# Relative-position rows written in eight pieces at a later place, and a new order of the feed-forward chunks, in a two-block transformer kernel

## The chip, the cores and the metric

The kernel runs on one core of a Trainium2 chip. The metric is the time of one execution on the device in microseconds (us); lower is better. Each measurement is the median of several runs.

## The reference, cut to what matters

Two transformer blocks run one after the other on 256 positions of width 2048, all in fp32. The first has a causal convolution branch, attention with a forgetting gate, gates, and a feed-forward part of width 8192. The second has attention with a relative-position bias, a pooling branch, and a gated feed-forward part of width 5632 with a short convolution. What the change touches:

```python
# first block
h = rmsnorm(x, g_mlp)
u = square(relu(h @ w_ff1))                  # 2048 -> 8192
x = x + u @ w_ff2                            # 8192 -> 2048
# second block
bias_own = rel_bias[:, rel_bucket(q_pos - k_pos)]        # 8 heads, 32 buckets
s_own = where(q_pos >= k_pos, q @ k.T * scale + bias_own, NEG)
...
u = h @ w_up                                 # 2048 -> 2 * 5632
gate, val = split(conv_b + causal_conv3(u, conv_w))
x = x + (silu(gate) * val) @ w_down          # 5632 -> 2048
```

The bias depends only on the head and on the distance of the two positions, so a row of 383 values for each head holds all of it, and a tile with one query per partition is that row shifted by one element from partition to partition.

## The kernel before, in words

**Chunks.** All the large products are one long list of chunks (`add_chunk`, line 137). A chunk makes 256 x 512 outputs in one PSUM tile (`acc`, two buffers). It has one weight tile of 512 x 512 for each 512 rows of the contraction, and each of these has four k steps of 128 rows. The activations stand transposed in tiles of the pool `kk` (11 buffers, line 79); they and the weights are split in a high and a low fp32r part, and a k step is three products (high-high, low-high, high-low) for two halves of the positions: six matmuls of 128x512 (`both`, line 882). A feed-forward chunk has four weight tiles, so 16 k steps.

**Weights.** `fetch` (line 831) loads a weight tile of 1 MB from SP's queue into one of four `raw` buffers, four tiles ahead of its use. `split_unit` (line 840) splits half a tile (a unit, two k steps) three units ahead: ScalarE casts (`wh`, line 846), VectorE subtracts (`wl`, line 847). The main loop (line 898) emits for each unit the split of a later unit, at the second unit of a tile also a fetch, then the two k steps.

**Tasks.** Everything else is emitted between k steps. The variable `now` counts k steps; `later(delay, fn)` (line 93) puts a function in a heap with a due time, and after every k step `run_due` (line 107) emits at most three that are due, the earliest due first and, of equal ones, the one put in first. `chain` (line 97) puts in several with a gap between. `need(key)` (line 112) runs tasks until a key is ready. The order of emission is the order in which each engine's queue runs; engines and queues wait on one another only through the data. `before[i]` runs a function where chunk i begins.

**Feed-forward, first block** (lines 787 to 793). Four times: four chunks of the first layer, `u0` to `u3` and so on, each from the four `f` tiles; then four chunks of the second layer, each of which takes the four `u` tiles in order, and each of which is added into x. A `u` chunk is emptied by `evac_ff` (line 559): ScalarE applies Relu, a task one step later squares, tasks from two steps later on transpose on VectorE (`turned`, line 180: 16 transposes, three to a task, line 190), and `split_out` (line 147) writes the high part on ScalarE (line 155) and the low part on VectorE (line 162). So the fourth `u` tile is made while the second layer's first chunk already uses the first three. `close_block` after the last of these blocks makes the second block's activations.

**Feed-forward, second block** (lines 811 to 820): the same shape with pairs of chunks (gate and value) of `w_up` that make `d0` to `d10`, in groups of 4, 4 and 3, and four `w_down` chunks behind each group.

**Relative-position rows** (lines 629 to 645). At k step 40, in the first block's projections, POOL's queue loads a one-hot table `oh` (33 x 384) and the bias table `rb` (33 x 8). 18 steps later a matmul `p_b` (line 638) makes the 8 rows of 383 values, VectorE copies them to `e` (8 partitions, line 640), and one DMA from POOL's queue (line 642) writes each row 128 times to DRAM, 1024 rows in all, with a stride of 513 floats for the shift. Much later `rel_bias_tiles` (line 647, called from the second block's `k2_done`) reads them back with a stride of 512 as bias tiles `k_nb`, four DMAs from POOL's queue.

Of the kernel before, what the change touches and what calls it, by code (L numbers as in the profile page):

```python
# [11 lines left out]
F32 = mybir.dt.float32  # L12
# [7 lines left out]
P = 128  # L20
# [3 lines left out]
NH = 8  # L24
W1 = 1024
FF1 = 8192
FF2 = 5632
EPS = 1e-6
NEG = -1e30
CW = 512  # L30
# [31 lines left out]
def tile_two_blocks(  # L62
# [5 lines left out]
    nc = tc.nc  # L68
    V, S, TE = nc.vector, nc.scalar, nc.tensor

    def pool(name, bufs, space=None):
        kw = {"space": space} if space else {}
        return ctx.enter_context(tc.tile_pool(name=name, bufs=bufs, **kw))
# [7 lines left out]
    s_p = pool("s", 2)  # L81
    pt_p = pool("pt", 3)
    bg_p = pool("bg", 2)
    st_p = pool("st", 4)
    dr_p = pool("dr", 1, DRAM)
# [7 lines left out]
    def later(delay, fn, *keys):  # L93
        seq[0] += 1
        heapq.heappush(tasks, (now[0] + delay, seq[0], fn, keys))

    def chain(delay, stages, *keys, gap=1):

        for i, fn in enumerate(stages):
            later(delay + i * gap, fn, *(keys if i == len(stages) - 1 else ()))  # L100
# [11 lines left out]
    def need(*keys):  # L112
        for key in keys:
            while key not in ready:
                run_one()
# [19 lines left out]
    chunks, before = [], {}  # L135

    def add_chunk(w, row0s, c0, ncol, acts, evac):

        chunks.append((w, row0s, c0, ncol, acts, evac))
# [61 lines left out]
    def group_keys(key):  # L201
        return [f"{key} {j}" for j in range(4)]
# [21 lines left out]
    def squares(part, n):  # L224
        for tb in range(TB):
            junk = s_p.tile([P, CW], F32, tag="s", name="junk")
            S.activation(junk, xs[n][:, tb, :], AF.Square, accum_out=part[:, tb, n:n + 1])  # L227
# [13 lines left out]
    def to_acts(name, n, gcol, delay):  # L241

        key = f"{name}{n}"
        def use(b, p):
            return split_out(key, 2 * b, 2, p, [gcol[:, 4 * n + 2 * b + i:4 * n + 2 * b + i + 1] for i in range(2)])
        if name == "h" or n == 3:
            transposed(xs[n], use, delay if name == "h" else delay + 3, group_keys(key), lag=0, step=0)
        else:
            turned(xs[n], use, delay, group_keys(key), rate=2, lag=3)
# [53 lines left out]
    AT = {}  # L303
# [73 lines left out]
    hT = lambda name: [f"{name}{n}" for n in range(4)]  # L377
# [57 lines left out]
    def evac_scaled(rname, then, mult=None):  # L435

        def evac(acc):
            z = z_p.tile([P, TB, CW], F32, tag="z", name="z")
            for tb in range(TB):
                S.activation(z[:, tb, :], acc[:, tb, :], AF.Copy, scale=R[rname][:, tb:tb + 1])  # L440
            then(z)
        return evac
# [94 lines left out]
    def evac_add(n, then=None):  # L537
        def evac(acc, tb=None):
            if tb is not None:
                V.tensor_tensor(out=xs[n][:, tb, :], in0=xs[n][:, tb, :], in1=acc, op=OP.add)  # L540
                nc.sync.dma_start(outr[:, tb, n * CW:(n + 1) * CW], xs[n][:, tb, :])
                return
            V.tensor_tensor(out=xs[n], in0=xs[n], in1=acc, op=OP.add)
            if then:
                then(n)
        return evac

    def next_acts(name, gfn, part, rname):
        def then(n):
            if n == 0:  # L550
                need("vcol")
            to_acts(name, n, gfn(), 2)
            squares(part, n)
            if n == 3:
                R[rname] = rstd_of(part, rname)
        return then


    def evac_ff(key):
        def evac(acc):  # L560
            z = z_p.tile([P, TB, CW], F32, tag="z", name="z_f")
            for tb in range(TB):
                S.activation(z[:, tb, :], acc[:, tb, :], AF.Relu, scale=R["r2"][:, tb:tb + 1])
            later(1, lambda: S.activation(z, z, AF.Square))
            turned(z, lambda b, p: split_out(key, 2 * b, 2, p), 2, group_keys(key))
        return evac
# [44 lines left out]
    def k2_done(half):  # L611
# [14 lines left out]
                head_task(2, h, 12 + 7 * i)  # L626
        return then

    def rel_bias_rows():
        oh = s_p.tile([33, 384], F32, tag="s", name="oh")  # L630
        nc.gpsimd.dma_start(oh, cst[0:33, C_OH:C_OH + 384])
        rb = const.tile([33, NH], F32, name="rb")
        nc.gpsimd.memset(rb[32:33, :], 1.0)
        nc.gpsimd.dma_start(rb[0:32, :], rel_bias_2.rearrange("h b -> b h"))

        def task():
            p = tr_p.tile([P, 512], F32, tag="tr", name="p_b")
            TE.matmul(p[0:8, 0:384], rb, oh, start=True, stop=True)
            e = s_p.tile([NH, 384], F32, tag="s", name="e")
            V.tensor_copy(e, p[0:8, 0:384])  # L640
            ed = dr_p.tile([NH, P * CW], F32, name="ed")
            nc.gpsimd.dma_start(bass.AP(tensor=ed.tensor, offset=ed.offset, ap=[[P * CW, NH], [CW + 1, P], [1, 383]]),
                                e[:, None, 0:383].to_broadcast([NH, P, 383]))
            AT["ed"] = ed
        later(18, task, "ed")

    def rel_bias_tiles():
        need("ed")
        ed = AT["ed"]
        for half in range(2):  # L650
            nb = k_p.tile([P, 4, MAXCOL], F32, tag="k", name="k_nb")
            o = ed.offset + half * 4 * P * CW + 127
            for c0, o, n in ((0, o + P, P), (P, o, T)):
                nc.gpsimd.dma_start(nb[:, :, c0:c0 + n],
                                    bass.AP(tensor=ed.tensor, offset=o, ap=[[CW, P], [P * CW, 4], [1, n]]))
            AT[2, "nb", half] = nb

    def v2_done(half):
# [70 lines left out]
    def evac_up(which, j, key):  # L729
        def then(z):  # L730
            cv = z_p.tile([P, 4, T], F32, tag="z", name="z_cv")

            def use(b, p):
                a = cv[:, 2 * b:2 * b + 2, :]
                c0 = (0 if which == "g" else 44) + 4 * j + 2 * b
                steps = conv3(a, p, lambda i, t: ccol[:, t, c0 + i:c0 + i + 1], lambda i: ccol[:, 3, c0 + i:c0 + i + 1])
                if which == "v":
                    g = FU["g", j][:, 2 * b:2 * b + 2, :]
                    need(f"gate{j} {2 * b}")
                    return steps + [lambda: V.tensor_tensor(out=a, in0=a, in1=g, op=OP.mult), *split_out(key, 2 * b, 2, a)]  # L740
                t = {}

                def sigmoid():
                    t["s"] = s_p.tile([P, 2, T], F32, tag="s", name="sg")
                    S.activation(t["s"], a, AF.Sigmoid)
                return steps + [sigmoid, lambda: V.tensor_tensor(out=a, in0=a, in1=t["s"], op=OP.mult)]
            if which == "g":
                FU["g", j] = cv
            if which == "g":
                turned(z, use, 2, group_keys(f"gate{j}"), rate=2)  # L750
            else:
                soon = j == FF2 // CW - 1
                transposed(z, use, 2 if soon else 3, group_keys(key), gap=1 if soon else 2)
        return then
# [4 lines left out]
    G4 = [0, 512, 1024, 1536]  # L759
# [24 lines left out]
    for n in range(4):  # L784
        add_chunk(w_mix_out[0], G4, n * CW, CW, hT("mg"),
                  evac_add(n, next_acts("f", lambda: vcol[:, VEC["g_mlp"], :], part1, "r2")))
    for blk in range(4):
        for i in range(4):
            j = 4 * blk + i
            add_chunk(w_ff1[0], G4, j * CW, CW, hT("f"), evac_ff(f"u{j}"))  # L790
        for n in range(4):
            add_chunk(w_ff2[0], [(4 * blk + i) * CW for i in range(4)], n * CW, CW, [f"u{4 * blk + i}" for i in range(4)],
                      evac_add(n, close_block if blk == 3 else None))
    wi2 = w_in_2[0]
    for half in range(2):
        add_chunk(wi2, G4, 2 * W1 + half * CW, CW, hT("i"), v2_done(half))
# [11 lines left out]
    def store(n):  # L808
        nc.sync.dma_start(outr[:, :, n * CW:(n + 1) * CW], xs[n])

    j = 0
    for cnt in (4, 4, 3):
        js = list(range(j, j + cnt))
        j += cnt
        for jj in js:
            add_chunk(w_up_2[0], G4, jj * CW, CW, hT("g"), evac_scaled("r4", evac_up("g", jj, f"d{jj}")))
            add_chunk(w_up_2[0], G4, FF2 + jj * CW, CW, hT("g"), evac_scaled("r4", evac_up("v", jj, f"d{jj}")))
        for n in range(4):
            add_chunk(w_down_2[0], [jj * CW for jj in js], n * CW, CW, [f"d{jj}" for jj in js],
                      evac_add(n, store if j == 11 else None))  # L820


    wtiles = []
# [53 lines left out]
        later(4 * n + 3, lambda n=n: squares(part0, n))  # L877
    later(16, first_rstd, "r1")
    later(18, load_vectors)
    later(40, rel_bias_rows)  # L880

    def both(k, kt, wh, wl, stop):

# [77 lines left out]
```

## Time and profile before

| | us |
|---|---|
| median of 3 runs | 2394.24 (2393.58 to 2395.01) |
| the profiled execution | 2393.52 |
| its span in the trace | 2391.8 |
| TensorE (PE) busy in it | 2362.4 |
| VectorE (DVE) busy | 1662.8 |
| ScalarE (ACT) busy | 1159.0 |
| GpSimd (POOL) busy | 36.7 |

The profile is one execution; times in it are us from its first instruction unless ns is said. PE is TensorE's matmuls, PEld its weight loads, DVE is VectorE, ACT ScalarE, SP the engine whose queue issues most DMAs (SPq). `L847` is line 847 of the kernel. A tile is named as in the program, so `acc<-wh,k_u` is a matmul into `acc` from the weights' high part and a `u` tile. In brackets behind an instruction stands the idle time of its engine ahead of it and what ended it. The end of a matmul is modelled, so that one of 128x512 shows a mean of 389 ns, though the next can start earlier. PEclk is the share of TensorE's full clock of 2.4 GHz that was granted; a half is 1.2 GHz.

### The profile page before, as it was taken

To read this page: it belongs to the slowest core of one execution; us is meant where nothing else is said; L and a number is where in the kernel's file an instruction comes from. 1 tells how busy PE (TensorE), PEld (TensorE's weight loads), DVE (VectorE), ACT (ScalarE), POOL (GpSimd) and SP (SyncE) were. 2 spreads that over 40 slices of the span, in tenths; PEclk is the share of its full clock that TensorE was granted. 3 is DMA by queue.
4 is the path that set the end of the run, shared out by engine and by line. 5 is a ranking of instruction groups with operands and counts; after the bars stand their busy time and mean duration, and the time that the engine had idled before them with its cause. 6 is when DMAs were issued, how large, how long until landed. Compare 5 with 4: busy or idle time off the path is not lost.

```text
span 2391.8 us, 27807 instructions
## 1 busy us (share of the span) xinstructions
PE 2362.4 (99%) x10649; PEld 1960.1 (82%) x10649; DVE 1662.8 (70%) x2293; ACT 1159.0 (48%) x1514; POOL 36.7 (2%) x53
## 2 busy tenths in 40 slices
PE   9899999999999999999999999999999999999999
PEld 9688888888888888888888888888888888888887
DVE  5487776665877567567578857668788568864884
ACT  5355454444455344344354455545555345554553
POOL 1000000000000000000000001000000000000000
PEclk9999999999999999999999999999999999999999
DMA  7755656655556556656555666555555656565553
GB/s 259 188 184 165 204 194 207 202 201 177 192 195 195 193 181 206 193 184 201 193 183 190 189 205 203 165 176 194 183 177 199 199 180 206 178 198 189 194 185 132
DMA packets 230966, 456.67 MB, mean 191 GB/s; under 512 B 8085, under 2 KB 15997, under 8 KB 230832
## 3 DMA queue, kind: packets, MB, share of 16 engines
q1 hardware_dynamic: 227584, 445.81, 56.7%
q0 software_dynamic: 3248, 9.08, 1.6%
q8 instruction: 83, 1.36, 0.2%
q14 instruction: 51, 0.42, 0.0%
HBM read 451.18 MB, written 3.67 MB: 190 GB/s over the span
## 4 chain that ended last, share of the span: by engine, by line
PE 91%; DVE 4%; DMA 2%; ACT 1%; issue 1%; SPq 0%; POOL 0%; ACTq 0%; DVEq 0%
PE acc L887 89%; DMA raw<-in_w_in_dram 2%; DVE wl L847 2%; DVE z_t L190 1%; ACT wh L846 1%; PE p_t L175 1%; PE acc_last L887 0%; DVE z_cv L484 0%; PE p_t L360 0%; PE p_s L316 0%; PE p_t L714 0%; DVE k_i L165 0%; PE p_p L351 0%; ACT junk L227 0%; DMA bg<-in_g_final_dram 0%
## 5 line engine op out<-in xcount | busy, mean ns | idle before, releaser
L847 DVE TENSOR_TENSOR wl<-raw,wh 128x1024 fp32r<-128x1024 f32 (+1 forms) x848 | 1021.6, 1214 | 635.1 <-ACT wh L846 546.5
L846 ACT CAST wh<-raw 128x1024 fp32r<-128x1024 f32 (+1 forms) x848 | 876.5, 1044 | 713.6 <-PE acc L887 648.9
L887 PE MATMUL acc<-wh,k_g 128*128 128x512 f32 x1408 | 378.4, 390 | 0.0
L887 PE MATMUL acc<-wh,k_h 128*128 128x512 f32 (+1 forms) x1344 | 352.2, 384 | 12.6 <-ACT wh L846 12.2
L887 PEld LDWEIGHTS acc<-wh,k_g 128*128 128x128 f32 x1408 | 263.0, 188 | 53.8
L887 PEld LDWEIGHTS acc<-wh,k_h 128*128 128x128 f32 x1344 | 247.2, 189 | 58.3 <-ACT wh L846 13.5
L887 PE MATMUL acc<-wh,k_u 128*128 128x512 f32 x1024 | 274.8, 390 | 4.5 <-DVE k_u L162 4.5
L887 PE MATMUL acc<-wh,k_f 128*128 128x512 f32 x1024 | 273.9, 389 | 0.0
L887 PEld LDWEIGHTS acc<-wh,k_u 128*128 128x128 f32 x1024 | 191.9, 188 | 45.9 <-DVE k_u L162 6.2
L887 PEld LDWEIGHTS acc<-wh,k_f 128*128 128x128 f32 x1024 | 192.1, 188 | 39.8
L887 PE MATMUL acc<-wl,k_g 128*128 128x512 f32 x704 | 216.9, 389 | 0.0
L887 PE MATMUL acc<-wl,k_h 128*128 128x512 f32 (+1 forms) x672 | 201.1, 380 | 0.1
L887 PE MATMUL acc<-wh,k_d 128*128 128x512 f32 x656 | 176.3, 390 | 1.5 <-DVE k_d L162 1.5
L887 PE MATMUL acc<-wl,k_u 128*128 128x512 f32 x512 | 157.7, 389 | 0.0
L887 PE MATMUL acc<-wl,k_f 128*128 128x512 f32 x512 | 157.6, 389 | 0.0
L887 PEld LDWEIGHTS acc<-wl,k_g 128*128 128x128 f32 x704 | 132.1, 188 | 27.8
L190 DVE STREAM_TRANSPOSE z_t<-z 32x256 f32<-32x256 f32 x336 | 146.3, 435 | 5.6
L887 PEld LDWEIGHTS acc<-wh,k_d 128*128 128x128 f32 x656 | 122.6, 188 | 27.1 <-DVE k_d L162 1.9
L887 PEld LDWEIGHTS acc<-wl,k_h 128*128 128x128 f32 x672 | 125.0, 188 | 23.6 <-DVE wl L847 0.7
L887 PE MATMUL acc<-wh,k_i 128*128 128x512 f32 x512 | 141.0, 398 | 0.6 <-ACT wh L846 0.6
L190 DVE STREAM_TRANSPOSE z_t<-z_f 32x256 f32<-32x256 f32 x256 | 111.4, 435 | 4.1
L887 PEld LDWEIGHTS acc<-wl,k_u 128*128 128x128 f32 x512 | 96.1, 188 | 20.0
(227 smaller groups left out, 2006.3 us busy)
## 6 DMA issues: line engine op xcount, KB each, us to landing
raw<-in_w_ff_dram SPq DMA_DIRECT2D x128, 1024.0 KB, 5.2
raw<-in_w_in_dram SPq DMA_DIRECT2D x104, 1024.0 KB, 5.1
raw<-in_w_up_dram SPq DMA_DIRECT2D x88, 1024.0 KB, 5.1
raw<-in_w_down_dram SPq DMA_DIRECT2D x44, 1024.0 KB, 5.2
raw<-in_w_mix_out_dram SPq DMA_DIRECT2D x16, 1024.0 KB, 5.1
raw<-in_w_out_dram SPq DMA_DIRECT2D x16, 1024.0 KB, 5.1
raw<-in_w_conv_out_dram SPq DMA_DIRECT2D x8, 1024.0 KB, 5.2
raw<-in_w_attn_out_dram SPq DMA_DIRECT2D x8, 1024.0 KB, 5.3
```

Of the source, the lines that this page charges most:

```text
L175: TE.transpose(p[:, j, tb * P:(tb + 1) * P], z[:, tb, (2 * b + j) * P:(2 * b + j + 1) * P], ident)
L190: V.transpose(dst, src)
L846: S.copy(wh[:, :, 0:ncol], raw)
L847: V.tensor_tensor(out=wl[:, :, 0:ncol], in0=raw, in1=wh[:, :, 0:ncol].bitcast(F32), op=OP.subtract)
L887: TE.matmul(halves[tb][:, 0:ncol], k[:, i, kt, tb * P:(tb + 1) * P], w[:, kk, 0:ncol], start=begin and first and kt == 0, stop=end and stop)
```

## The change

Two edits. The first makes the relative-position rows in another form and at another place. The task's matmul now has 128 columns of weights (`rbw`, each head's column 16 times, copied by VectorE in the task itself), so that the rows come out on 128 partitions, 16 for each head; `e` has 128 partitions; and eight DMAs from SP's queue, 20 k steps apart, write 128 rows each. They fill the same 1024 rows of DRAM, 513 floats apart. The loads of `oh` and `rb` and the task go from k step 40 to where the second chunk of the first feed-forward layer begins. The second edit puts one chunk (or one pair of chunks) of the next feed-forward block ahead of the second layer of each block but the last, in both transformer blocks.

```diff
@@ -626,33 +626,41 @@
                 head_task(2, h, 12 + 7 * i)
         return then
 
+    ROW = CW + 1
+
     def rel_bias_rows():
+
         oh = s_p.tile([33, 384], F32, tag="s", name="oh")
         nc.gpsimd.dma_start(oh, cst[0:33, C_OH:C_OH + 384])
         rb = const.tile([33, NH], F32, name="rb")
         nc.gpsimd.memset(rb[32:33, :], 1.0)
         nc.gpsimd.dma_start(rb[0:32, :], rel_bias_2.rearrange("h b -> b h"))
+        per = P // NH
 
         def task():
+            rbw = st_p.tile([33, NH, per], F32, tag="rbw", name="rbw", bufs=1)
+            V.tensor_copy(rbw, rb[:, :, None].to_broadcast([33, NH, per]))
             p = tr_p.tile([P, 512], F32, tag="tr", name="p_b")
-            TE.matmul(p[0:8, 0:384], rb, oh, start=True, stop=True)
-            e = s_p.tile([NH, 384], F32, tag="s", name="e")
-            V.tensor_copy(e, p[0:8, 0:384])
-            ed = dr_p.tile([NH, P * CW], F32, name="ed")
-            nc.gpsimd.dma_start(bass.AP(tensor=ed.tensor, offset=ed.offset, ap=[[P * CW, NH], [CW + 1, P], [1, 383]]),
-                                e[:, None, 0:383].to_broadcast([NH, P, 383]))
-            AT["ed"] = ed
-        later(18, task, "ed")
+            TE.matmul(p[:, 0:384], rbw.rearrange("b h i -> b (h i)"), oh, start=True, stop=True)
+            e = s_p.tile([P, 384], F32, tag="s", name="e")
+            V.tensor_copy(e, p[:, 0:384])
+            ed = AT["ed"] = dr_p.tile([NH, P * ROW], F32, name="ed")
+
+            def write(k):
+                nc.sync.dma_start(bass.AP(tensor=ed.tensor, offset=ed.offset + k * ROW, ap=[[NH * ROW, P], [1, 383]]),
+                                    e[:, 0:383])
+            chain(2, [lambda k=k: write(k) for k in range(P // per)], "ed", gap=20)
+        later(18, task)
 
     def rel_bias_tiles():
         need("ed")
         ed = AT["ed"]
         for half in range(2):
             nb = k_p.tile([P, 4, MAXCOL], F32, tag="k", name="k_nb")
-            o = ed.offset + half * 4 * P * CW + 127
+            o = ed.offset + half * 4 * P * ROW + 127
             for c0, o, n in ((0, o + P, P), (P, o, T)):
                 nc.gpsimd.dma_start(nb[:, :, c0:c0 + n],
-                                    bass.AP(tensor=ed.tensor, offset=o, ap=[[CW, P], [P * CW, 4], [1, n]]))
+                                    bass.AP(tensor=ed.tensor, offset=o, ap=[[CW, P], [P * ROW, 4], [1, n]]))
             AT[2, "nb", half] = nb
 
     def v2_done(half):
@@ -784,13 +792,23 @@
     for n in range(4):
         add_chunk(w_mix_out[0], G4, n * CW, CW, hT("mg"),
                   evac_add(n, next_acts("f", lambda: vcol[:, VEC["g_mlp"], :], part1, "r2")))
+    def ff1_chunk(j):
+        if j == 1:
+            before[len(chunks)] = rel_bias_rows
+        add_chunk(w_ff1[0], G4, j * CW, CW, hT("f"), evac_ff(f"u{j}"))
+
+    for j in range(4):
+        ff1_chunk(j)
     for blk in range(4):
-        for i in range(4):
-            j = 4 * blk + i
-            add_chunk(w_ff1[0], G4, j * CW, CW, hT("f"), evac_ff(f"u{j}"))
+        mine = range(4 * blk, 4 * blk + 4)
+        if blk < 3:
+            ff1_chunk(4 * blk + 4)
         for n in range(4):
-            add_chunk(w_ff2[0], [(4 * blk + i) * CW for i in range(4)], n * CW, CW, [f"u{4 * blk + i}" for i in range(4)],
+            add_chunk(w_ff2[0], [j * CW for j in mine], n * CW, CW, [f"u{j}" for j in mine],
                       evac_add(n, close_block if blk == 3 else None))
+        if blk < 3:
+            for j in range(4 * blk + 5, 4 * blk + 8):
+                ff1_chunk(j)
     wi2 = w_in_2[0]
     for half in range(2):
         add_chunk(wi2, G4, 2 * W1 + half * CW, CW, hT("i"), v2_done(half))
@@ -808,16 +826,19 @@
     def store(n):
         nc.sync.dma_start(outr[:, :, n * CW:(n + 1) * CW], xs[n])
 
-    j = 0
-    for cnt in (4, 4, 3):
-        js = list(range(j, j + cnt))
-        j += cnt
-        for jj in js:
-            add_chunk(w_up_2[0], G4, jj * CW, CW, hT("g"), evac_scaled("r4", evac_up("g", jj, f"d{jj}")))
-            add_chunk(w_up_2[0], G4, FF2 + jj * CW, CW, hT("g"), evac_scaled("r4", evac_up("v", jj, f"d{jj}")))
+    def up_chunks(j):
+        add_chunk(w_up_2[0], G4, j * CW, CW, hT("g"), evac_scaled("r4", evac_up("g", j, f"d{j}")))
+        add_chunk(w_up_2[0], G4, FF2 + j * CW, CW, hT("g"), evac_scaled("r4", evac_up("v", j, f"d{j}")))
+
+    up_chunks(0)
+    for j0, j1 in ((0, 4), (4, 8), (8, 11)):
+        for j in range(j0 + 1, j1):
+            up_chunks(j)
+        if j1 < 11:
+            up_chunks(j1)
         for n in range(4):
-            add_chunk(w_down_2[0], [jj * CW for jj in js], n * CW, CW, [f"d{jj}" for jj in js],
-                      evac_add(n, store if j == 11 else None))
+            add_chunk(w_down_2[0], [j * CW for j in range(j0, j1)], n * CW, CW, [f"d{j}" for j in range(j0, j1)],
+                      evac_add(n, store if j1 == 11 else None))
 
 
     wtiles = []
@@ -877,7 +898,6 @@
         later(4 * n + 3, lambda n=n: squares(part0, n))
     later(16, first_rstd, "r1")
     later(18, load_vectors)
-    later(40, rel_bias_rows)
 
     def both(k, kt, wh, wl, stop):
 
```

## Rows read from the trace of the kernel before

**Rows 1.** The page's first part: busy us, share of the span, instructions.

```profile
PE 2362.4 (99%) x10649; PEld 1960.1 (82%) x10649; DVE 1662.8 (70%) x2293; ACT 1159.0 (48%) x1514; POOL 36.7 (2%) x53
```

**Rows 2.** Waits of PE: us in total, times, longest us.

```profile
PE acc L887 <- ACT wh L846: 12.9, 3, 11.1
PE acc L887 <- DVE k_u L162: 4.5, 4, 1.1
PE p_t L360 <- ACT pt L355: 1.9, 1, 1.9
PE acc L887 <- DVE k_d L162: 1.5, 1, 1.5
...
PE p_s L315 <- ACT k_qk L372: 0.5, 1, 0.5
```

**Rows 3.** The chain that ended last, in order of time: start, length, what.

```profile
86.88 31.05 DMA raw<-in_w_in_dram
...
762.93 168.52 PE acc L887 x742
```

**Rows 4.** Timeline around the stall at 105 us: start, length, instruction, [idle before].

```profile
92.58 1.05 ACT L846 CAST wh<-raw 128x1024 fp32r<-128x1024 f32 x1 [3.15 <-DMA raw<-in_w_in_dram]
...
115.29 2.00 ACT L846 CAST wh<-raw 128x1024 fp32r<-128x1024 f32 x2 [12.90 <-DMA raw<-in_w_in_dram]
...
116.39 2.07 PE L887 MATMUL acc<-wh,k_h 128*128 128x512 f32 x4 [11.09 <-ACT wh L846]
```

**Rows 5.** DMA issues: queue, count, KB each, median us from issue to landing.

```profile
raw<-in_w_ff_dram SPq DMA_DIRECT2D x128, 1024.0 KB, 5.2
...
ed<-e POOLq DMA_DIRECT2D x1, 1532.0 KB, 37.4
...
out_dram<-x SPq DMA_DIRECT2D x2, 256.0 KB, 2.0
...
oh<-in_cst_dram POOLq DMA_DIRECT2D x1, 49.5 KB, 4.6
```

**Rows 6.** Windows: length, busy of PE, PEld, DVE, ACT, POOL; PEclk, DMA share, GB/s.

```profile
755.00:763.00 8.00, 6.86 (x31) 5.35 (x30) 6.24 (x11) 3.56 (x5) 0.00 (x0) 1.00 0.42 131
...
1282.00:1291.00 9.00, 7.88 (x35) 6.20 (x34) 7.27 (x12) 3.99 (x5) 0.00 (x0) 1.00 0.47 133
116.39:121.17 4.78, 4.78 (x13) 3.77 (x14) 3.57 (x3) 4.03 (x6) 0.00 (x0) 0.57 0.66 231
1495.81:1499.50 3.69, 3.69 (x12) 2.90 (x11) 2.02 (x6) 2.66 (x7) 0.00 (x0) 0.54 0.79 273
...
701.00:723.00 22.00, 22.00 (x99) 18.23 (x98) 17.85 (x27) 11.28 (x13) 0.00 (x0) 1.00 0.59 193
```

**Rows 7.** The page's costliest groups: busy, mean ns of one, idle before.

```profile
L887 PE MATMUL acc<-wh,k_f 128*128 128x512 f32 x1024 | 273.9, 389 | 0.0
```

**Rows 8.** Timeline of PE, DVE, SP and ACT in the first feed-forward chunks.

```profile
704.06 1.07 PE L887 MATMUL acc<-wh,k_f 128*128 128x512 f32 x4
...
703.77 1.23 DVE L847 TENSOR_TENSOR wl<-raw,wh 128x1024 fp32r<-128x1024 f32 x1 [2.15 <-PE acc L887]
...
700.52 0.37 SPq L837 DMA_DIRECT2D raw<-in_w_ff_dram  x1
...
705.03 0.37 SPq L837 DMA_DIRECT2D raw<-in_w_ff_dram  x1
...
718.81 0.37 SPq L837 DMA_DIRECT2D raw<-in_w_ff_dram  x1
...
731.01 1.06 ACT L846 CAST wh<-raw 128x1024 fp32r<-128x1024 f32 x1 [1.66 <-PE acc L887]
```

**Rows 9.** Instructions of tiles p_b and e: ns min/median/max, first and last start.

```profile
L638 PE MATMUL p_b<-oh,rb x2: 482/484/486, 74.2 to 74.5; 33*8 33x384 f32 x2
...
L640 DVE COPY e<-p_b x1: 545/545/545, 75.0 to 75.0; 8x384 f32<-8x384 f32 x1
```

**Rows 10.** Timeline of POOL ahead of the first feed-forward chunks.

```profile
663.26 0.72 POOL L215 TENSOR_TENSOR r<-sv,ehalf 128x2 f32<-128x2 f32 x1 [155.33 <-DVE sv L214]
```

## The prediction, made before the changed kernel was run

> **What bounds the kernel now.** I read the page's engine line first: PE is busy 2362.4 us of a span of 2391.8 [rows 1], so only about 29 us can be won without taking matmuls away, and the change takes none away. The question is which of these 29 us belong to the two places that it touches. The list of PE's waits answers most of that [rows 2]. One wait of 11.1 us, for ScalarE's cast of a weight tile, is the largest by far. Four waits of 1.1 us each are for the low part of a `u` tile, that is, for the last feed-forward activation. One of 1.5 us is for a `d` tile.
>
> The large one is a late transfer. The chain of waits has 31 us of weight load there [rows 3]. In the timeline the cast waits 3.15 us for its weights at 92.6 and 12.9 us at 115.3, and PE is idle 11.09 us up to 116.4 [rows 4]. The transfer list shows what else was on the way: the relative-position rows, issued just before, took 37.4 us to land, where a weight tile takes 5.2 [rows 5]. Behind the stall PEclk is 0.57 for 4.78 us, so the matmuls there run near the lower level of 1.2 GHz [rows 6].
>
> **The change part by part.** The pace of an undisturbed stretch is 168.52 us for 742 matmuls, 0.227 us each [rows 3]. A matmul's modelled length is 0.389 us [rows 7], so an idle time that the trace shows hides another 0.389 - 0.227 = 0.16 us.
>
> *The one large write goes from 75 us.* The stall is 11.09 + 0.16 = 11.25 us [rows 4]. In the slow stretch 13 matmuls take 4.78 us [rows 6]; at 0.227 they would take 2.95, so 1.83 us more. PE's wait of 0.5 us for `k_qk`, shortly after [rows 2], comes while VectorE and ScalarE have lost their lead over PE through the stall; I count it as gone, 0.5, with 0 and 0.7 as its ends. Sum 13.6 us. The end on the other side: the loads at 92.6 were already 3.15 us late [rows 4], and other transfers of POOL's queue are on the way then too; if that lateness were theirs and stayed, 3.15 us less would be won. I take it as the large write's.
>
> *Feed-forward of the first block.* The windows around the first and last boundary lose 8.00 - 6.86 = 1.14 and 9.00 - 7.88 = 1.12 us [rows 6], four alike [rows 2]. What is late is the chain of the fourth `u` tile: Relu, square, 16 transposes, high part, low part. With a whole chunk (96 matmuls, 21.8 us) between this tile and the second layer's first use of it, that chain has more than enough time. Next in line are `u0` to `u2`, which are older still. Three of four boundaries get such a chunk, each worth 1.14 + 0.16 = 1.30: 3.9 us. The last has no next block and keeps its wait. The tiles held at once become nine (four `f`, five `u`) of eleven buffers, so no buffer wait comes in. VectorE is busy 17.85 of 22 us in a first-layer chunk [rows 6]; five such chunks in a row run at that rate as four did.
>
> *Feed-forward of the second block.* PE waits for a `d` tile once, 1.5 us [rows 2], and that is at the last group, which gets no chunk ahead. The two boundaries that change show no wait: 0 us. If the cover went (VectorE late there), the price would be that of one such wait, 1.5 us, twice.
>
> *The task at its new place.* It comes due 18 k steps into the second `u` chunk, so behind the second k step of the third. PE gets there at 704.06 [rows 8]. The weights `rbw` of its matmul are now made by VectorE in the same task, behind the subtraction that starts at 703.77 and takes 1.23 [rows 8], so not before 705.0. The copy itself (33x128) has no row; I take 0.25 us, under the 0.545 of the 8x384 copy [rows 9]. PE waits until about 705.25: 1.2 us, new. Queued behind it on PE are the third chunk's matmuls, all of them. Ends: 0 if VectorE is ahead, and 3.5 us if the copy and the subtraction come one subtraction (1.23) later and the clock falls as it did after the wait of 1.9 us at 1495 (PEclk 0.54 for 3.69 us, 12 matmuls that would take 2.72, so 0.97 more) [rows 2, 6, 8]. After waits of 1.14 PEclk stayed at 1.00 [rows 6], so I count none. The matmul and the copy to `e` keep their free size of 384, and only move [rows 9].
>
> *SP's queue.* Eight issues of 0.37 us are added, between fetches that are 24 matmuls, some 5.5 us, apart. The first waits for `e`: the matmul ends near 706.0, the copy near 706.6. SP has done the fetch of 700.52 and would issue the next at 705.03 [rows 8]; that one goes at about 707.0, 2 us late. The shortest distance here from a fetch to its first cast is 731.01 - 718.81 = 12.2 us [rows 8], and 5.2 of it are the landing [rows 5], so 7.0 us of lateness cost nothing. Later pieces find `e` ready.
>
> *The pieces on the DMA engines.* A piece is 196 KB. A store of 256 KB from SP lands in 2.0 us; an eighth of the old write is 37.4 / 8 = 4.7 us [rows 5]. Both ends are under 7.0, so 0 us. I take the lower, as it has the same queue and 128 partitions too. The engines are 0.59 busy [rows 6], so the 27 us (20 steps of six matmuls) between two pieces leave 11 us to catch up.
>
> *POOL's queue.* The loads of `oh` and `rb` (4.6 us) [rows 5] go where POOL has nothing behind its step at 663.26 [rows 10], 40 us ahead of their use: 0 us; if that lead were gone, those 4.6.
>
> Sum: 13.6 + 3.9 - 1.2 = 16.3 us less. The profiled execution took 2393.52, so 2377.2 on its own scale; the median of the runs stands 0.7 higher, which gives 2377.9. I put the forecast between, 2377.5.
>
> **The rivals.**
>
> *The pieces give the gain back (no change).* Eight pieces hold the loads up eight times. At 2.0 us each that is 16 us, and PE pays it all only if the loads have no slack to absorb it: 2377.5 + 16 = 2393.5. Against it stand the 7.0 us of slack and the 11 us to catch up between pieces. A page of the Trainium skill speaks for it: "DMA: Bandwidth & Descriptors", Bandwidth, says to batch transfers to 1 MiB or more, and its fit of some 2.0 us fixed per transfer would make eight pieces cost an estimated 19.6 us where one write costs 5.6. By that rule the old form was the good one; the trace has 37.4 us for it [rows 5], so it does not hold here for the write that goes. Chance 4%.
>
> *Each piece holds the loads as the whole write did (slower).* Its place is SP's own queue, where the next weight load stands right behind a piece. If its 128 rows were handled as slowly as the old 1024, each piece would bring a stall like the one at 105 us, 11.25 + 1.83 = 13.1 us, so 8 x 13.1 = 105 us: 2482. It decides from the point where a piece delays loads by 7.0 + 16.3 / 8 = 9.0 us, almost twice its share of the old write, 4.7. What speaks for it is that no row shows rows of 1532 bytes going from SP; against it the store's 2.0 us [rows 5]. Chance 4%.
>
> *The boundaries keep their waits.* If what is late there is VectorE as a whole and not the one tile, the 3.9 us stay: 2381.4. The 17.85 of 22 us [rows 6] leave VectorE room, and the wait names `k_u`. Chance 9%.
>
> *The early loads stay late.* The 3.15 us above remain: 2380.7. Chance 8%.
>
> **How the numbers follow.** The forecast has 75%, the rivals 4, 4, 9 and 8%. The low end is the forecast without the new wait (2376.3) and with the runs' scatter of 0.7 twice: 2375.0. The high end takes in either small rival (3.9 or 3.15) together with the dear end of the new wait (2.3 more than counted): 2384.0, rounded up. A measurement of this kernel can tell about 0.2%, 4.8 us, from no change; both small rivals and their sum lie beyond that on the fast side, so faster is 75 + 9 + 8 = 92%, within 4%, slower 4%.
>
> **What would show it.** In the profile after, PE's waits have no 11.1 us for a cast and one `k_u` wait of 1.1 us in place of four; PEclk has no slow stretch near 117; a new wait of about 1.2 us on `p_b` for `rbw` stands near 690 (703 less the 13 won before); `ed<-e` has eight issues from SP that land in 2 to 5 us each, and no cast waits for weights near them; `k_d` keeps its 1.5. A cast that waits for `raw` behind each piece would prove the prediction wrong, and so would `k_u` waits at all four boundaries, or a second stall ahead of 120 us.

## The result, and the profile after

The changed kernel takes 2376.78 us (median of four runs, 2374.96 to 2377.29), the kernel before, measured with it, 2393.91. The ratio is 0.9929, with a 95% interval of 0.9916 to 0.9941: 17.1 us less, where the forecast was 2377.5 us, 16.3 less. The span of the profiled execution went from 2391.8 to 2375.0. One of the eleven runs of the kernel with the new order alone took 3509.91 us at a granted clock of 0.632, and its numbers below leave that run out.

The list of PE's waits of the changed kernel, to be held against [rows 2] (us in total, times, longest):

```profile
PE p_t L360 <- ACT pt L355: 1.9, 1, 1.9
PE acc L907 <- ACT wh L867: 1.8, 2, 1.1
PE acc L907 <- DVE k_d L162: 1.5, 1, 1.5
PE acc L907 <- DVE k_u L162: 1.1, 1, 1.1
...
PE p_b L644 <- DVE rbw L642: 1.0, 1, 1.0
...
PE p_s L315 <- ACT k_qk L372: 0.2, 1, 0.2
```

The 11.1 us for a cast are gone (what is left of that line are two small waits that the kernel before has too, 1.1 us at the start and 0.7 where the second block begins), three of the four waits for `k_u` are gone, the wait for `k_d` stayed, and a new one for `rbw` has come. The wait for `k_qk` shrank from 0.5 to 0.2.

The windows of the changed kernel, of the same kind as [rows 6]: the stretch of the old stall, the first boundary, the last boundary, and the place of the new task:

```profile
102.00:123.00 21.00, 20.84 (x93) 16.77 (x92) 17.83 (x26) 11.88 (x14) 0.00 (x0) 1.00 0.58 201
744.00:752.00 8.00, 8.00 (x37) 6.64 (x36) 6.27 (x9) 4.76 (x6) 0.00 (x0) 1.00 0.54 171
1268.00:1276.00 8.00, 6.88 (x30) 5.36 (x29) 5.87 (x8) 5.03 (x6) 0.00 (x0) 1.00 0.52 173
685.00:707.00 22.00, 21.04 (x91) 16.72 (x90) 16.85 (x27) 10.13 (x12) 0.00 (x0) 1.00 0.56 186
```

PE is busy through the first two but for 0.16 us, at a clock of 1.00; the last boundary still loses 8.00 - 6.88 = 1.12 us; the new task loses 22.00 - 21.04 = 0.96.

The timelines of PE, VectorE and SP at the new task show the wait and the place of the pieces in SP's queue, as forecast from [rows 8]:

```profile
690.63 0.91 PE L644 MATMUL p_b<-oh,rbw 33*128 33x384 f32 x2 [0.96 <-DVE rbw L642]
...
689.22 1.23 DVE L868 TENSOR_TENSOR wl<-raw,wh 128x1024 fp32r<-128x1024 f32 x1 [2.16 <-PE acc L907]
690.36 0.21 DVE L642 COPY rbw<-rb 33x128 f32<-33x128 f32 x1
691.58 0.56 DVE L646 COPY e<-p_b 128x384 f32<-128x384 f32 x1 [1.00 <-PE p_b L644]
...
692.16 0.35 SPq L650 DMA_DIRECT2D ed<-e  x1
...
714.33 0.37 SPq L858 DMA_DIRECT2D raw<-in_w_ff_dram  x1
714.75 0.50 SPq L650 DMA_DIRECT2D ed<-e  x1
```

The copy to `rbw` stands right behind the subtraction for a weight tile, and PE waits for it. The second piece is issued 0.42 us behind a weight load. The transfer list shows the landing, here the median of the eight:

```profile
ed<-e SPq DMA_DIRECT2D x8, 191.5 KB, 6.9
```

A piece could take 2.0 to 4.7 us by the prediction's bounds; the median is 6.9. The first piece goes out 6.20 us after the load before it, which has landed by then, and lands in 3.3 us. Each of the other seven stands right behind a load of 1 MB, which itself takes 5.2, and they land in 5.9 to 7.6.

### The profile page after: what moved, and what is told of

Read it like the earlier page. It is cut to its first block, busy times and chain, and to the rows that moved or that the text cites. A ratio compares the mean times of both kernels' runs of the same rounds, so it can differ in the third digit from the quotient of the medians.

```text
span 2375.0 us, 27814 instructions
## 1 busy us (share of the span) xinstructions
PE 2360.5 (99%) x10649; PEld 1961.1 (83%) x10649; DVE 1662.1 (70%) x2294; ACT 1156.8 (49%) x1514; POOL 35.5 (1%) x52
## 4 chain that ended last, share of the span: by engine, by line
PE 96%; DVE 2%; ACT 1%; issue 1%; DMA 0%; SPq 0%; POOL 0%; ACTq 0%; DVEq 0%; POOLq 0%
PE acc L907 93%; DVE wl L868 1%; PE p_t L175 1%; ACT wh L867 0%; PE acc_last L907 0%; DVE z_t L190 0%; DVE z_cv L484 0%; PE p_t L360 0%; PE p_s L316 0%; PE p_t L722 0%; PE p_p L351 0%; DMA gm_rows<-in_g_mix_dram 0%; PE p_s L315 0%; PE p_t L361 0%; DMA bg<-in_g_final_dram 0%
```

## The experiments

**One edit at a time.** The first kernel has the rows' edit in the old order of chunks, the second the new order with the old write.

```diff
 # e1_rows_only: the kernel before, with the new rel_bias_rows
-    later(40, rel_bias_rows)
...
             j = 4 * blk + i
+            if j == 1:
+                before[len(chunks)] = rel_bias_rows
 # e2_order_only: the changed kernel's two chunk loops, old rel_bias_rows at later(40, ...)
-        if j == 1:
-            before[len(chunks)] = rel_bias_rows
```

> The rows' edit alone, in the chunk order of before. My theory: the two edits are independent, and this one is worth the stall near 105 us (11.25 us idle, 1.83 of half clock, some 0.3 of the wait behind it) less the new wait of PE for rbw (1.1): 12 to 13 us under the kernel before, ratio about 0.995; PE's list shows no 11.1 us for a cast and still four waits of 1.1 us for k_u. Rival: the edits depend on each other (the pieces only find room because the new order spreads VectorE's and SP's work); then a cast waits for weights near a piece, and the gain is under 10 us.

> The order's edit alone, with the one large write where it was. My theory: three of four waits for k_u go, 1.30 us each, and the second transformer block gives nothing: 3.9 us under the kernel before, ratio about 0.998; the 11.1 us for a cast stays. Rival one: waits move to another tile, the gain is 0. Rival two: the second block's order also counts, gain over 5 us.

The rows alone: 2379.35 us against 2392.84, ratio 0.9943 (0.9931 to 0.9956), 13.5 us less. The order alone: 2389.12, ratio 0.9983 (0.9974 to 0.9993), 3.7 us less. The sum, 17.2, is what both do together (17.1). PE's waits in the two, first lines:

```profile
PE acc L896 <- DVE k_u L162: 4.5, 4, 1.1
PE acc L896 <- ACT wh L856: 2.1, 2, 1.1
```

```profile
PE acc L898 <- ACT wh L857: 13.3, 3, 11.3
PE p_t L360 <- ACT pt L355: 1.9, 1, 1.9
PE acc L898 <- DVE k_d L162: 1.5, 1, 1.5
PE acc L898 <- DVE k_u L162: 1.1, 1, 1.1
```

Each edit takes away its own wait and leaves the other's. As far as these times can tell, the edits are independent. The second block's order was not run by itself, but no wait went there: the 1.5 us for `k_d` are left.

**The new wait, and the boundaries that are left.** The third kernel makes `rbw` in a task of its own, six k steps ahead of the matmul. The fourth also puts the whole first layer of the last feed-forward block ahead of the second layer of the block before it, in both transformer blocks.

```diff
 # e3_rbw_early, on the changed kernel
         def task():
-            rbw = st_p.tile([33, NH, per], F32, tag="rbw", name="rbw", bufs=1)
-            V.tensor_copy(rbw, rb[:, :, None].to_broadcast([33, NH, per]))
...
+        def widen():
+            AT["rbw"] = st_p.tile([33, NH, per], F32, tag="rbw", name="rbw", bufs=1)
+            V.tensor_copy(AT["rbw"], rb[:, :, None].to_broadcast([33, NH, per]))
+        later(12, widen)
 # e4_all_ahead, on top of it
         if blk < 3:
-            ff1_chunk(4 * blk + 4)
+            for j in range(4 * blk + 4, 4 * blk + (8 if blk == 2 else 5)):
+                ff1_chunk(j)
...
-        if blk < 3:
+        if blk < 2:
             for j in range(4 * blk + 5, 4 * blk + 8):
...
-        for j in range(j0 + 1, j1):
+        for j in range(j0 + 1, j1) if j0 < 8 else ():
             up_chunks(j)
         if j1 < 11:
-            up_chunks(j1)
+            for j in range(j1, j1 + 1 if j1 == 4 else 11):
+                up_chunks(j)
```

> The changed kernel with the copy that makes rbw in a task six k steps ahead of the matmul. My theory: the wait for rbw (1.0 us in PE's list) is the task's own order, so it goes whole, and the time falls by 1.1 us against the changed kernel, 18 us under the kernel before. Rival: VectorE is late there whatever it is given, and the same microsecond comes back as a wait of the matmuls behind p_b for wl or of p_b for something else; then no difference from the changed kernel.

> As the run with rbw early, and in both transformer blocks the whole first layer of the last feed-forward block goes ahead of the second layer of the block before it, so that the last boundaries have cover too; eleven of eleven activation buffers are then in use. My theory: the last k_u wait (1.1 shown, 1.3 real) and the k_d wait (1.5 shown, 1.7 real) go as well: some 4 us under the changed kernel, 21 us under the kernel before, ratio about 0.991. Rival: with all buffers held the u15 or d10 tile waits for a buffer and the wait only moves; then as the run with rbw early, 18 us.

With `rbw` early: 2374.42 us, ratio 0.9923 (0.9911 to 0.9936). That interval overlaps the changed kernel's, so the microsecond itself is seen in the trace alone: no wait on `p_b` is left. The span is 2372.4 against 2375.0, but not all of these 2.6 us are the wait's, as the last section shows from the clock. With all the first layers ahead: 2370.99 us, ratio 0.9907 (0.9893 to 0.9920), 3.4 us under the run with `rbw` early on the same chip, and the runs of the two do not overlap (2370.17 to 2371.88, 2373.78 to 2377.81). The two spans, 2372.4 and 2369.3, differ by 3.1 us, about the 1.3 and 1.7 that the expectation counts for the two waits. PE's longest waits there:

```profile
PE acc L912 <- ACT wh L872: 2.0, 2, 1.1
PE p_t L360 <- ACT pt L355: 1.9, 1, 1.9
PE warm L887 <- DVE ehalf L125: 1.1, 1, 1.1
PE p_t L175 <- ACT z L440: 1.0, 3, 0.5
```

No wait for `k_u` or `k_d` is left, and none for a buffer has come, though all eleven are in use. This version beats the kernel before. All its runs are below those of the changed kernel too (2374.96 to 2377.29), though the intervals of the two ratios touch (0.9893 to 0.9920 and 0.9916 to 0.9941).

**What made the old write dear: its place, its size or its form?** The edit changes all three at once, so eight kernels, all with the new chunk order, take them apart. First the old form (8 partitions, one DMA, POOL's queue) at the new place, and the new form's pieces at the old place:

```diff
 # e5_old_form_late: the changed kernel with the old rel_bias_rows, still at the second ff1 chunk
 # e6_pieces_early: the changed kernel
-        if j == 1:
-            before[len(chunks)] = rel_bias_rows
...
+    later(40, rel_bias_rows)
...
-            e = s_p.tile([P, 384], F32, tag="s", name="e")
+            e = pt_p.tile([P, MAXCOL], F32, tag="pt", name="e")
```

> The new chunk order and the new place (second chunk of the first feed-forward layer), but the old form: rows on 8 partitions and one write of 1024 rows from POOL's queue. Theory form: the write is slow in itself, wherever it stands; it again takes some 30 us or more to land, a cast waits for weights near 710 us and PE stands some 8 to 12 us: about 2387. Theory place: it was the crowd of transfers at 70 to 80 us that made the stall; here the DMA engines are 0.59 busy and nothing else of POOL is on the way, so no wait: about 2375 (without the wait for rbw).

> The changed kernel with the task back at k step 40 and the eight pieces from SP spread from there (e lies in a buffer of the pt pool, so that it does not hold one that the attention heads want). Theory form and theory size: no cast waits for weights, 2376 to 2378. Theory place: casts wait for weights near 75 to 110 us, 3 us or more: over 2379.

The old form at the new place: 2388.94 us, ratio 0.9980 (0.9970 to 0.9990). The pieces at the old place: 2375.32, ratio 0.9926 (0.9911 to 0.9940). Of the old form at the new place, PE's waits and the transfer list:

```profile
PE acc L899 <- ACT wh L859: 11.5, 3, 9.8
```

```profile
ed<-e POOLq DMA_DIRECT2D x1, 1532.0 KB, 37.1
```

The write takes 37.1 us where it took 37.4 [rows 5], and the stall, now 9.8 us, has moved with it to 722 us. So the place is not what made the write dear; the old place is even a little better, for PE's list has no wait for `rbw` there. Now the size and the queue, all at the old place, with `e` in the pool `pt`:

```diff
 # e7_one_early_sp and e10_one_early_pool: one DMA in place of the eight pieces
-            chain(2, [lambda k=k: write(k) for k in range(P // per)], "ed", gap=20)
+            def write():
+                nc.sync.dma_start(bass.AP(tensor=ed.tensor, offset=ed.offset,      # e10: nc.gpsimd
+                                          ap=[[NH * ROW, P], [ROW, P // per], [1, 383]]),
+                                  e[:, None, 0:383].to_broadcast([P, P // per, 383]))
+            chain(2, [write], "ed")
 # e11_one8_sp and e12_one16_sp: one DMA from SP with per = 1 and per = 2, so 8 and 16 partitions (patterns to match)
 # e8_old_form_pieces_early and e9_old_form_pieces_sp: 8 partitions, eight DMAs of 16 rows of each head (e9: ROW for CW)
+            def write(k):
+                nc.gpsimd.dma_start(bass.AP(tensor=ed.tensor, offset=ed.offset + 16 * k * (CW + 1),   # e9: nc.sync
+                                            ap=[[P * CW, NH], [CW + 1, 16], [1, 383]]),
+                                    e[:, None, 0:383].to_broadcast([NH, 16, 383]))
+            chain(2, [lambda k=k: write(k) for k in range(8)], "ed", gap=20)
```

> As the pieces at the early place, but one DMA from SP with all 1024 rows, 8 from each of 128 partitions. Theory form (8 partitions are what is slow): it lands in under 15 us, and PE waits at most 2 us: 2376 to 2379. Theory size (1.5 MB in one go ahead of the loads is too much): a stall of 8 us or more, over 2384.

> One DMA of all 1024 rows, 8 from each of 128 partitions, early place, from POOL's queue in place of SP's. Theory form: the queue does not matter, it lands in under 20 us and no cast waits over 3 us: 2374 to 2377. Theory queue (POOL's transfers take turns with the loads and SP's do not): a stall as before, 8 us or more, over 2383.

> One DMA of all 1024 rows from 8 partitions, as the old one but from SP's queue, early place, new chunk order. Theory form: it is slow from any queue, lands in 20 us or more, and as the loads stand behind it on the same queue PE stalls 8 us or more: over 2383. Theory queue: it is POOL's queue that makes it slow; from SP it lands in under 15 us and PE does not wait: 2374 to 2377.

> The same from 16 partitions (each head's row twice, 64 writes from each partition). If the number of partitions that are read sets the speed in proportion, it lands in about half the time of the one from 8, with a stall of a few us or none; if 8 against 16 decides how many DMA engines take part, its rows go as fast as those from 128 partitions, and it lands within 3 us of that one's 12.3, with no stall: 2374 to 2377.

| rows from | queue | landing, us | longest wait of PE for a cast, us | median, us | ratio (interval) |
|---|---|---|---|---|---|
| 128 partitions | SP | 12.3 | 1.1 | 2375.03 | 0.9924 (0.9909 to 0.9939) |
| 128 partitions | POOL | 14.3 | 1.1 | 2374.91 | 0.9923 (0.9908 to 0.9938) |
| 16 partitions | SP | 18.2 | 1.4 | 2374.68 | 0.9923 (0.9908 to 0.9938) |
| 8 partitions | SP | not in the list | 13.8 | 2391.38 | 0.9990 (0.9980 to 0.9999) |

One undivided write from 128 partitions costs PE no wait, from either queue. From 8 partitions it costs the stall, from SP a little more of it than from POOL. Sixteen are enough for PE, but only just: in ScalarE's waits of that run a cast waits 7.4 us for its weights, which the splits made ahead absorb.

```profile
ACT wh L866 <- DMA raw<-in_w_in_dram: 10.1, 3, 7.4
```

The windows show the difference; the first fence is the write from 8 partitions, then 16, then 128, all from SP and all in the 6 us from 82 us on (columns as in [rows 6]):

```profile
82.00:88.00 6.00, 6.00 (x28) 4.99 (x27) 2.88 (x5) 3.26 (x4) 0.00 (x0) 1.00 0.50 56
```

```profile
82.00:88.00 6.00, 6.00 (x28) 4.95 (x28) 2.89 (x4) 3.26 (x4) 0.00 (x0) 1.00 0.91 101
```

```profile
82.00:88.00 6.00, 6.00 (x28) 4.96 (x27) 2.88 (x5) 3.26 (x4) 0.00 (x0) 1.00 1.04 209
```

With 8 partitions half of the DMA engines' time is busy (0.50) and 56 GB/s move; with 16 it is 0.91 and 101 GB/s; with 128 it is 1.04 and 209 GB/s, some of it weight loads. The Trainium skill, "DMA: Bandwidth & Descriptors", in the section on why a DMA increments its semaphore by 16, says that the number of engines of a transfer is the largest up to 16 that divides the slowest dimension of both sides. That gives 8 engines for 8 partitions and 16 for the other two, and the busy shares agree. It looks as if the number of engines made the write slow. But if it did, the expectation says, 16 partitions would land within 3 us of the 12.3 that 128 take. They took 18.2, about half of the 37.4 that 8 take from POOL's queue, as the expectation has it for a speed in proportion to the partitions.

The last two runs cut the old form in eight.

> The new chunk order, the early place and the old form on 8 partitions, but in eight DMAs of 128 rows from POOL's queue, 20 k steps apart (e in the pt pool). Theory form, as far as it says that a slow form hurts in any size: loads are late near each piece and some casts wait, over 2379. Theory size: an eighth of the old write holds the loads up by some 4 to 5 us, under the 7 us of slack, so no wait: 2375 to 2377; the pieces alone would then have been enough.

> The old form on 8 partitions in eight DMAs of 128 rows, now from SP's queue, where each stands behind weight loads that pace it (early place, new chunk order, e in the pt pool). Theory pacing: eight pieces spread over 220 us hold the loads up by an eighth of the old write each, 4 to 5 us, under the slack of 7; no stall, 2374 to 2377, so that the pieces alone would have been enough had they come from SP. Theory form alone: a slow form hurts in any size, casts wait near each piece, over 2379.

From POOL's queue: 2385.78 us, ratio 0.9970 (0.9958 to 0.9982). From SP's: 2374.02, ratio 0.9921 (0.9906 to 0.9935). The first result looks as if a slow form hurt in any size, but the timelines of the two queues say otherwise; first POOL's in the one, then SP's in the other:

```profile
75.72 4.78 POOL L645 DMA_DIRECT2D ed<-e  x8 [2.47 <-DVE e L640]
86.16 0.59 POOL L505 DMA_DIRECT2D bg<-in_b_gate_dram  x1 [5.65 <-DMA ed<-e]
```

```profile
75.50 0.35 SPq L650 DMA_DIRECT2D ed<-e  x1
75.95 27.51 SPq L857 DMA_DIRECT2D raw<-in_w_in_dram  x5
103.51 0.40 SPq L650 DMA_DIRECT2D ed<-e  x1
```

POOL issued all eight within 4.78 us: nothing in its queue waits for PE, so the 20 k steps between them in the program set no time. So this run has no pieces spread in time, which its expectation is about, and PE waited 8.9 us at most. On SP's queue each piece stands behind weight loads that wait for buffers, so the second goes 28 us after the first, and PE waits at most 1.1 us for a cast. Eight pieces of the old form are enough, then, on a queue that something paces. Whether POOL's queue would do as well, with pieces that are really spread, was not run.

The run on POOL's queue also decides between partitions and engines. This is its window from 88 us on, with several of the eight DMAs on the way at once:

```profile
88.00:94.00 6.00, 6.00 (x28) 4.95 (x28) 5.90 (x11) 2.11 (x2) 0.56 (x1) 1.00 0.97 54
```

Nearly all of the engines' time is busy (0.97), and still only 54 GB/s move, no more than the 56 of one write from 8 partitions with half of it busy. What the rate follows is the number of partitions that are read: 54 / 8 = 6.8 and 56 / 8 = 7.0 GB/s for each of 8, and 101 / 16 = 6.3 for each of 16. From 128 it is 209 / 128 = 1.6, so there something else is the limit. What it is on the way out of a partition that sets the rate, no run here shows.

## Why the prediction was right, and where its sizes were off

*The stall of the large write.* Counted at 13.6 us with the wait behind it; less the new wait, 12.4 for the rows' edit. That edit alone measured 13.5, with an interval from 10.5 to 16.5. Of the 0.5 for `k_qk`, 0.2 stayed, so the term was 13.4. That this wait came from the stall is not shown: with the order alone PE stands 11.3 us and has no such wait in its list, and with the write from 8 partitions on SP's queue it stands 13.8 and has 0.2. The rest of the difference is below what the runs can tell.

*The boundaries.* 3.9 us forecast, 3.7 measured with the order alone (1.7 to 6.2), three waits of four gone. The run with all first layers ahead shows the cause: cover at the last boundary takes the last `k_u` wait away too.

*The second block's order.* Forecast 0; the waits show none gone.

*The new wait.* Forecast 1.2 us, from the subtraction's end plus a copy taken at 0.25. The copy took 0.21, the idle time shown is 0.96, and 0.96 + 0.16 = 1.1 us. The clock did not fall (1.00).

*The pieces.* This is the step that was off in size. Taken at 2.0 us to land, with 4.7 as the dear end; measured 6.9. The sentence took the store at the kernel's end as the nearest row, but no weight load stands ahead of that store, while seven of the pieces queue behind one. It did no harm, since what counts is how late the loads behind them come, and the queue ahead does not add to that: in the trace's single DMA packets the 128 rows of a piece are through in 0.7 to 1.6 us, less than the 2.0 that was taken. That kept within the slack of 7.0: from 685 to 900 us no cast waits for weights.

*The rivals.* The two about the pieces fell with that: no stall at any of the eight. "The early loads stay late" fell too: from 60 to 130 us no cast of the changed kernel waits for weights, where one waited 3.15 us at 92.6 [rows 4]. "The boundaries keep their waits" fell by the order alone.

*What the prediction did not see* is which part of the rows' edit mattered. It argued from the write's 37.4 us as one price. The experiments split it: the place did not make the write dear, the division in pieces was not needed, and 16 or 128 partitions in place of 8 would have done alone. Nor was an eighth of 37.4 us, 4.7, the right price for a piece of the old form: spread on SP's queue such a piece is through in 1.6 to 2.6, as the last section shows.

## What to carry to other kernels

A transfer from few partitions can starve the loads beside it, whether the mean busy share of the DMA engines looks moderate (0.50 with 56 GB/s) or full (0.97 with 54 GB/s): lay the source out on more partitions first (16 were just enough here, 128 had room), and only then think of cutting it up or moving it. Pieces that the program puts on a queue at intervals are spread in time only if something else on that queue waits; on POOL's idle queue all eight went within 4.78 us. And where the last link of a chain is late by a microsecond at each block boundary, a chunk of independent work put ahead of the boundary takes the whole wait away, as long as the buffers reach.

## What was not expected of the hardware

The rate of a write depends on its length too, and not only on the number of partitions. One DMA from 8 partitions on SP's queue made PE wait 13.8 us, whereas eight DMAs of the same rows from the same 8 partitions and the same queue, the first two 28 us apart, cost PE nothing that it could feel. The trace's single DMA packets, one for each row of 1532 bytes, show why. The undivided write sends 109 rows in its first 2 us, 74 of them in under 0.1 us each; from then on a row takes about 0.22 us and 65 go in 2 us, so that the last is through at 109.4 us, 30.7 after the first. A piece of 128 rows lies almost wholly in the fast beginning: its median row takes 0.065 us, and the eight pieces take 1.6 to 2.6 us each. So short writes go faster by themselves and do not only hide in the loads' slack. Why the beginning is fast, no run here shows. From 16 to 128 partitions the landing went only from 18.2 to 12.3 us.

The same write from 8 partitions cost more on SP's queue (PE waits 13.8 us) than on POOL's (11.1 to 11.3). That fits the order of a queue, since on SP the loads stand behind the write, but no run here separates that from the rest.

The wait of 1.9 us for `pt` stands in every kernel's list, but the clock falls behind it only in some traces. The first line is the changed kernel just after that wait, the second the one with `rbw` early around it:

```profile
1479.72:1483.13 3.41, 3.41 (x10) 2.64 (x9) 1.75 (x4) 3.03 (x7) 0.00 (x0) 0.50 0.70 265
1477.00:1482.00 5.00, 4.68 (x22) 3.94 (x23) 3.33 (x6) 3.23 (x8) 0.00 (x0) 1.00 0.64 210
```

The changed kernel's trace has such a stretch near its start as well (PEclk 0.50 from 8.57 to 11.99 us), and the other has 1.00 there. In the kernel before, such a stretch of 3.69 us for 12 matmuls [rows 6] costs 0.97 us against their undisturbed pace, so the 2.6 us between these two spans are the wait for `rbw` and the clock together.
